# The context tile first in attention's last v part, the queries' rope table behind it, and unread products at the front of a hybrid block

## The chip, the cores and the metric

The kernel runs on one core of one Trainium2 chip. The metric is the device time of one execution in microseconds (us), the median over the runs shown. A core has TensorE (PE in the profile, its weight loads PEld), VectorE (DVE), ScalarE (ACT), GpSimd (POOL) and SyncE (SP), which issues the transfers between the main memory and the on-chip memory. Every engine works through its own list of instructions in order, and waits on semaphores for the others. TensorE writes into a small memory of eight banks (PSUM), from which VectorE and ScalarE fetch its results.

## The reference

One layer over 1024 latent tokens with a prefix of 256 context tokens, width 1024, batch 1, in float32:

```python
shift, scale, gate = split(silu(c) @ w_ada + b_ada, 3)          # and the same for c_ctx
h  = rms_norm(x)   * (1 + scale)   + shift
hc = rms_norm(ctx) * (1 + scale_c) + shift_c
qkv_a, z_a, a, b, q_b, k_b, v_b, z_b, gates = split_cols(h @ w_in)     # and of hc @ w_in
o_a = gdn_bidirectional(...)        # 8 heads of 128: short conv, gated delta rule, both directions
q = axial_rope(rms_norm(q_b)); k = concat(rms_norm(k_bc), axial_rope(rms_norm(k_b)))
v = concat(v_bc, v_b)
o_b = softmax(q0 k0) v - lam * softmax(q1 k1) v                 # 8 heads, two of 64 per head
y_a = rms_norm(o_a) * silu(z_a);  y_b = rms_norm(o_b) * (1 - lam0) * silu(z_b)
x = x + gate * ((g_a * (y_a @ w_oa) + g_b * (y_b @ w_ob)) @ w_out)
```

Rope turns pairs of a row's channels by an angle of the token's grid position; its cosines and sines, with the norm's gain in them, are a table that this kernel computes early, once for k and once for q, and keeps in the main memory (`tbd`).

## The kernel before, in words

All large products are made in three passes: each operand is split into a high part of fewer bits and a low part (the rest), and high x high, high x low, low x high are summed in a bank. `hs` holds the normalized, modulated h, transposed (channels on the partitions), as a high and a low tile for each of three groups of tokens: latent tiles 0 to 3, latent tiles 4 to 7, and the context's two tiles (group 2). `wh` and `wl` are a weight's high and low part, made from the raw load `wr`.

Before the program runs, a planner writes the order: each piece of work is a generator (a stream) that yields (engine, estimated us, what it depends on, what to emit), and `flow` or `turn_flow` picks the next step by the planner's own estimates of time. So a change of one stream can move the rows of others, and the engines then execute the order as it was written.

**The front** (`front`, L243) runs streams side by side. `loads` issues on SyncE: the constants `ct` (identity and two triangles, 128 x 384), c and c_ctx (`rows`), four tiles of x, the first weights, the first pair of w_ada's pieces (`wa`, 1 MB each), small vectors (`rw`), four tiles of x, three more pairs of `wa`, the context. `modulation` (L332) applies silu to c, transposes it (`tp<-ct,sil`), and for each of four pairs makes 8 small products of each piece (`mp<-wa,pad`, the "pads" below, each 32 columns of the array wide), copies the result (`mrow`; the first piece's on VectorE, the second's on ScalarE), and sums it by two "fold" products (`mp<-fold,mrow`), from which `mods` (shift and scale) comes. `rms` squares and sums each tile of x on ScalarE (`junk`), makes the inverse root on GpSimd and scales x on VectorE. `turns` transposes x (`pt<-ct,x`), and `turned` makes h's high part on ScalarE (`hs`, L407), h again on VectorE (`hf`, L410) and the low part on VectorE or GpSimd (L413). `main` (L417) makes the first 256 columns of the projection from them, the first `mm` products. `bank` (L238) hands out one of three banks for the front's transposes and modulation.

**The middle.** The convolution's projections follow, and then attention's k, v and q are projected in ten parts of 256 columns: four of k, two of v, four of q (`parts` in `run`), while the gated delta rule (GDN) runs beside them. `part_flow` (L937) makes the products of a part, two tiles of tokens (512 x 256 values, 48 products of 256 columns) at a time; k and v have ten tiles, the two of the context last, q has eight. `part_out` (L963) fetches a bank: for v a high and a low part (`vt`, L971 and L972), which SyncE stores (`vd`); for k and q a copy (`raw`), squares (`sq`). `part_post` (L989) then makes the norm's factor (`rsq`, L994, L995, and a power on GpSimd, L179) and six rope operations on VectorE (`sq`, `fin`, L1005 to L1007, two halves of three), four transposes on TensorE (`tr<-ct,fin`), two parts (`col`) and the stores (`qd`).

The queries' table is loaded into `hx`, whose buffer (tag `s20`) is that of the context's high part of h: its load (L947) must wait until the last product that reads the context is done. In the kernel before that is the last tile of the second v part, right ahead of the first q part. SyncE issues in order, so whatever stands behind a waiting request waits too.

Of the kernel before, what the change touches and what calls it, by code (L numbers as in the profile page):

```python
# [8 lines left out]
F32 = mybir.dt.float32  # L9
# [8 lines left out]
P = 128  # L18
D = 1024
KT = D // P  # L20
L = 1024
LC = 256
LT = L + LC
NT = LT // P
NL = L // P
# [9 lines left out]
PE, DVE, ACT, POOL, DMA, ADMA, DV2, PL1 = range(8)  # L35
# [8 lines left out]
class Block:  # L44
# [150 lines left out]
    def setup(self):  # L195
        nc, a = self.nc, self.a
        cp = self.cp = self.pool("const")
        self.dp = self.pool("spill", space=DRAM)
        ct = cp.tile([P, 3, P], F32, name="ct")
        nc.sync.dma_start(ct, a["consts"].rearrange("(a p) n -> p a n", p=P))  # L200
        self.ident, self.up, self.lo = (ct[:, i, :] for i in range(3))
        self.one = self.lo[:, 0:1]
        self.mhalf = cp.tile([P, 1], F32, name="mhalf")
        nc.gpsimd.memset(self.mhalf, -0.5)
        self.da = self.dp.tile([H, 2 * NT, 4, 32, 32], F32, name="da")
        self.db = self.dp.tile([H, 2 * NT, 4, 32, 32], F32, name="db")
        self.ya = self.dp.tile([2, H, P, L], F32, name="ya")
        self.yb = self.dp.tile([H, P, L], F32, name="yb")
        self.gkq = self.dp.tile([H, P, LT + L], F32, name="gkq")
        self.gkk = self.dp.tile([H, LT, P], F32, name="gkk")  # L210
        self.gv = self.dp.tile([H, LT, P], F32, name="gv")
        self.sza = self.dp.tile([H, P, L], F32, name="sza")
        self.szb = self.dp.tile([H, P, L], F32, name="szb")
        self.qd = self.dp.tile([2, H, P, L], F32, name="qd")
        self.kd = self.dp.tile([2, H, P, LT], F32, name="kd")
        self.vd = self.dp.tile([2, LT, H * P], F32, name="vd")
        self.gt = self.dp.tile([2 * KT, P, L], F32, name="gt")
        self.ma = self.dp.tile([KT, P, L], F32, name="ma")
        self.xq = self.dp.tile([H, P, 2, NT // 2, 2, 2, P], F32, name="xq")
        self.tbd = self.dp.tile([2, P, 1024], F32, name="tbd")  # L220
        self.gcd = self.dp.tile([2, H, LT], F32, name="gcd")
        self.gad = self.dp.tile([1, D], F32, name="gad")
        self.rbd = self.dp.tile([H, L], F32, name="rbd")
        for n in ("gkq", "gkk", "gv", "sza", "szb", "qd", "kd", "vd", "gt", "gcd", "ya", "yb"):
            self.dbg[n] = getattr(self, n).name
# [17 lines left out]
    def front(self, st, early, kv0):  # L243
# [5 lines left out]
        xt, wa, raws, T = {}, {}, {}, {}  # L249
# [82 lines left out]
        def modulation():  # L332
            sil = fs.tile([16, P], F32, name="sil")
            yield lambda: "rows" in T
            t = yield ACT, 0.3, T["rows"], lambda: nc.scalar.activation(sil, rows, AF.Silu), AF.Silu
            ib, tb, tp = self.bank("tp")
            t = yield PE, 0.2, [t, tb], lambda: self.tr(tp[:, 0:16], sil)
            tc = yield DVE, 0.15, [t], lambda: V.tensor_copy(cT, tp[:, 0:16])
            self.pfree.append((ib, tc))
            tz = yield PL1, 0.3, [], lambda: nc.gpsimd.memset(pad, 0.0)  # L340
            tc = yield DVE, 0.15, [tz, tc], lambda: V.tensor_copy(pad[:, :, 0:2].rearrange("p k s -> p s k"), c2)
            mrow = fs.tile([P, 2, W], F32, name="mrow")
            for u in range(4):
                yield lambda: ("wa", u, 0) in T and self.pfree
                ib, tb, mp = self.bank("mp")
                m = mods[:, :, 2 * u:2 * u + 2]
                bias = smallT[:, 0:16].rearrange("p (i k) -> p i k", i=2)[:, :, 2 * u:2 * u + 2]
                te = []
                for i in range(2):
                    yield lambda: ("wa", u, i) in T  # L350
                    o = i * W
                    for k in range(KT):
                        j = k % 4
                        t = yield PE, 0.08, [T["wa", u, i], tc, tb], lambda: self.mm(
                            mp[32 * j:32 * j + 32, o:o + W], pad[:, k], wa[u, i][:, k], k < 4, k >= 4)
                    if i:
                        t = yield ACT, 0.35, [t], lambda: nc.scalar.copy(mrow[:, i], mp[:, o:o + W])
                    else:
                        t = yield DVE, 0.42, [t], lambda: V.tensor_copy(mrow[:, i], mp[:, o:o + W])
                    for q in range(2):  # L360
                        t1 = yield PE, 0.17, [t], lambda: self.mm(
                            mp[:, o + 2 * q:o + 2 * q + 2], mrow[:, i, q * P:q * P + P], self.fold[:, 0:2])
                    te.append(t1)
                T["mm", u] = t
                yield lambda: "small" in T
                t = yield DVE, 0.17, [te, T["small"]], lambda: V.tensor_tensor(
                    m, mp.rearrange("p (i x) -> p i x", i=2)[:, :, 0:4].rearrange("p i (k s) -> p i k s", k=2),
                    bias.unsqueeze(3).to_broadcast([P, 2, 2, 2]), ALU.add)
                self.pfree.append((ib, t))
                T["m", u] = t  # L370
# [46 lines left out]
        def main():  # L417
            pts = [self.pm.tile([P, 512], F32, tag="mm", name="mm") for _ in range(5)]
            for g, ks in ORDER:
                n = len(groups[g]) * P  # L420
                for s, k in [(s, k) for s in range(2) for k in ks]:
                    yield lambda: ("h", g, k) in T and ("w", k // 4) in T
                    th, tl, _ = self.hsel(groups[g][0])
                    pt = pts[4][:, s * W:s * W + W] if g == 2 else pts[2 * s + g]
                    for i, (wt, ht) in enumerate(((0, th), (0, tl), (1, th))):
                        e = yield PE, 0.2265 if n == 512 else 0.1195, [T["h", g, k], T["w", k // 4]], lambda: self.mm(
                            pt, T["hl"][wt][:, k, s * P:(s + 1) * P], ht[:, k, :n], k == i == 0, k == KT - 1 and i == 2)
                    if k == KT - 1:
                        self.first_[s, g] = pt, e
            self.parts_done, self.part_t[0] = 1, e  # L430
# [506 lines left out]
    def part_flow(self, parts):  # L937

        self.free, self.nb = [None, None], 0
        free = self.free  # L940
        for i, (kind, pair) in enumerate(parts):
            yield lambda: i in self.parts_
            hi, lo, tw = self.parts_.pop(i)
            if parts[i - 1][0] != kind == "q":
                self.hx = self.hc.tile([P, 2, L], F32, tag="s20", name="hx")
                self.rope["q"] = self.hx[:, 0].rearrange("p (a b t f) -> p a b t f", a=2, b=2, f=32), (
                    yield DMA, 1.5, [self.part_t[i - 1]], lambda: self.nc.sync.dma_start(self.hx[:, 0], self.tbd[0]))  # L947
            for t0 in range(0, NL if kind == "q" else NT, 2):
                yield lambda: len(free) > self.nb
                pt = self.pm.tile([P, 512], F32, tag="mm", name="mm")  # L950
                for j in range(2):
                    th, tl, o = self.hsel(t0 + j)
                    m = 0
                    for k in range(KT):
                        for ht, wt in ((th, hi), (th, lo), (tl, hi)):
                            t = yield PE, 0.1195, [free[self.nb], tw], lambda: self.mm(
                                pt[:, j * W:j * W + W], ht[:, k, o:o + P], wt[:, k], m == 0, m == 3 * KT - 1)
                            m += 1
                self.evacs.append(self.part_out(kind, pair, t0, pt, t, free, self.nb))
                self.nb += 1  # L960
            self.parts_done, self.part_t[i] = i + 1, t

    def part_out(self, kind, pair, t0, pt, t, free, n):  # L963

# [24 lines left out]
    def part_post(self, kind, pair, t0, raw, sq, tr, t, s):  # L989

        nc, tk, V, Q = self.nc, self.tk, self.nc.vector, self.nc.gpsimd
        g, (tb, tt) = self.rope["g"], self.rope[kind]
        ss = self.rsq[:, t0:t0 + 2, 4 * pair:4 * pair + 4] if kind == "q" else tk.tile([P, 2, 4], F32, tag=f"ss{s}", name="ss")
        t = yield DVE, 0.6, [t], lambda: V.tensor_reduce(ss, sq.rearrange("p (t g d) -> p t g d", t=2, d=64), AX.X, ALU.add)  # L994
# [478 lines left out]
    def lam_setup(self):  # L1473
# [15 lines left out]
        self.dg = cp.tile([P, 1], F32, name="dg")  # L1489
        yield DVE, 0.15, [], lambda: V.tensor_scalar_mul(self.dg, self.diff_g, 1.0 - LAM0)  # L1490

    ISSUE = 0.5
    SPI = 0.5
    MW = 0.0
# [728 lines left out]
```

## Time and profile before

| | |
|---|---|
| three runs | 1931.37, 1928.17, 1931.5 us (median 1931.37) |
| the profiled execution | 1929.92 us, its span 1927.8 us |
| TensorE busy | 1885.5 us, 98% of the span |
| VectorE, ScalarE, GpSimd busy | 75%, 56%, 35% |
| the front (until the first transfers behind it) | 0 to 70 us |
| the v part that is changed, and the first q part | about 590 to 655 us |

A row of a timeline gives the start in us, the time from the group's first start to its last end in us, the engine, the line, the operation with output <- inputs, the partitions and shape, the count, and in brackets the idle time of the engine just before it and what ended it. A fp32 product of full precision stands there as two records. A row of the waits gives the engine and what it waited for, the total in us, the times and the longest. In the chain of waits a row is the start, the time and the piece. A row of a window gives its length, each engine's busy time (TensorE, its weight loads, VectorE, ScalarE, GpSimd) and instructions, the granted clock, the share of the transfer engines and GB/s.

### The profile page before, as it was taken

To read this page: it belongs to the slowest core of one execution; us is meant where nothing else is said; L and a number is where in the kernel's file an instruction comes from. 1 tells how busy PE (TensorE), PEld (TensorE's weight loads), DVE (VectorE), ACT (ScalarE), POOL (GpSimd) and SP (SyncE) were. 2 spreads that over 40 slices of the span, in tenths; PEclk is the share of its full clock that TensorE was granted. 3 is DMA by queue.
4 is the path that set the end of the run, shared out by engine and by line. 5 is a ranking of instruction groups with operands and counts; after the bars stand their busy time and mean duration, and the time that the engine had idled before them with its cause. 6 is when DMAs were issued, how large, how long until landed. Compare 5 with 4: busy or idle time off the path is not lost.

```text
span 1927.8 us, 37500 instructions
## 1 busy us (share of the span) xinstructions
PE 1885.5 (98%) x13807; PEld 1659.8 (86%) x13807; DVE 1446.3 (75%) x3613; ACT 1076.1 (56%) x2237; POOL 678.3 (35%) x610
## 2 busy tenths in 40 slices
PE   6999999999999999999999999999999999999999
PEld 4888888899999998888888888888997888888887
DVE  4697998957887887867865865338996979995677
ACT  4543444426233563677576656448885868884222
POOL 3200000005441342343333332326766667672203
PEclk9999999999999999999999999999999999999999
DMA  9144535575545557666785565666436474226542
GB/s 335 56 140 97 137 95 138 123 190 179 168 148 186 176 189 231 229 195 226 216 292 175 196 199 159 214 229 224 130 124 207 160 242 155 84 88 216 190 152 87
DMA packets 383039, 336.39 MB, mean 174 GB/s; under 512 B 142610, under 2 KB 323444, under 8 KB 381832
## 3 DMA queue, kind: packets, MB, share of 16 engines
q1 hardware_dynamic: 382855, 333.99, 55.2%
q8 instruction: 109, 1.79, 0.4%
q14 instruction: 75, 0.61, 0.1%
HBM read 222.14 MB, written 111.79 MB: 173 GB/s over the span
## 4 chain that ended last, share of the span: by engine, by line
PE 80%; DVE 7%; DMA 5%; ACT 4%; issue 2%; POOL 1%; SPq 1%; ACTq 0%; DVEq 0%; POOLq 0%
PE mm L56 40%; PE s L56 7%; PE v L56 5%; PE chain L56 5%; PE mb L56 5%; PE ma L56 4%; PE x L56 3%; PE t L63 3%; PE out L56 3%; PE gram L56 1%; DVE S L1579 1%; DMA sk<-gkq 1%; DVE ac L601 1%; PE tr L63 1%; PE mp L56 1%
## 5 line engine op out<-in xcount | busy, mean ns | idle before, releaser
L56 PE MATMUL mm<-hs,wh 128*128 128x512 f32 (+1 forms) x2048 | 648.6, 390 | 1.5 <-DVE hs L413 1.4
L56 PEld LDWEIGHTS mm<-hs,wh 128*128 128x128 f32 x2048 | 371.3, 189 | 58.9 <-DVE hs L413 1.9
L56 PE MATMUL mm<-hs,wl 128*128 128x512 f32 (+1 forms) x1024 | 397.6, 388 | 1.0 <-POOL wl L893 1.0
L56 PE MATMUL mm<-wh,hs 128*128 128x256 f32 (+1 forms) x1792 | 327.3, 283 | 0.3 <-ACT sq L985 0.3
L56 PEld LDWEIGHTS mm<-wh,hs 128*128 128x128 f32 x1792 | 276.8, 188 | 0.8 <-ACT sq L985 0.5
L1579 DVE TENSOR_SCALAR_CACHE_REDUCE S<-s,rsq 128x512 f32<-128x512 f32 (+1 forms) x384 | 239.5, 654 | 27.6 <-DMA vl<-vd 12.6
L56 PE MATMUL mm<-wl,hs 128*128 128x256 f32 (+1 forms) x896 | 253.3, 283 | 0.0
L1616 POOL TENSOR_TENSOR S<-S 128x1280 f32<-128x1280 f32 x64 | 189.1, 2958 | 91.9 <-ACT S L1609 90.6
L56 PEld LDWEIGHTS mm<-hs,wl 128*128 128x128 f32 x1024 | 193.9, 189 | 29.9 <-POOL wl L893 1.4
L1592 ACT ACTIVATE S<-S,mn 128x1280 f32<-128x1280 f32 x128 | 175.2, 1372 | 51.4 <-DVE mn L1591 51.3
L56 PEld LDWEIGHTS mm<-wl,hs 128*128 128x128 f32 x896 | 168.6, 188 | 0.1
L601 DVE SCALAR_TENSOR_TENSOR ac<-xc,convT,ac 128x1284 f32<-128x1284 f32 (+1 forms) x96 | 138.6, 1447 | 11.3 <-ACT ac L599 10.7
L56 PE MATMUL s<-kk,qh 128*128 128x512 f32 (+1 forms) x384 | 142.6, 372 | 1.9 <-DVE S L1579 1.7
L56 PE MATMUL s<-kk,ql 128*128 128x512 f32 (+1 forms) x384 | 133.0, 358 | 0.4 <-DMA ql<-qd 0.4
L1653 DVE TENSOR_TENSOR al<-t,ah 128x512 fp32r<-128x512 f32 (+1 forms) x192 | 106.8, 594 | 7.4 <-ACT ah L1648 6.0
L586 POOL MEMSET xc<- 128x2 f32 (+1 forms) x64 | 3.6, 101 | 297.3 <-ACT sq L635 113.8
L1167 DVE TENSOR_TENSOR ts<-ts,tmp 80x31 f32<-80x31 f32 (+15 forms) x248 | 92.2, 372 | 6.0
L1334 ACT ACTIVATE vd<-chain,edk 128x128 f32<-128x128 f32 x144 | 52.2, 370 | 76.9 <-PE chain L56 71.1
L56 PE MATMUL ma<-y,wh 128*128 128x512 f32 x256 | 93.0, 409 | 1.8 <-DVE g L1826 1.8
L1165 DVE TENSOR_TENSOR tmp<-ab,ts 80x31 f32<-80x31 f32 (+15 forms) x248 | 89.4, 360 | 6.4 <-DMA ab<-da 1.1
L1648 ACT CAST ah<-t 128x512 fp32r<-128x512 f32 (+1 forms) x192 | 88.1, 522 | 9.0 <-PE t L63 8.5
L56 PE MATMUL v<-al,vh 128*128 128x256 f32 x320 | 90.2, 282 | 0.7 <-DVE al L1653 0.6
(296 smaller groups left out, 4302.6 us busy)
## 6 DMA issues: line engine op xcount, KB each, us to landing
wr<-in_w_in_dram SPq DMA_DIRECT2D x48, 512.0 KB, 5.8
hx<-in_w_in_dram SPq DMA_DIRECT2D x64, 256.0 KB, 4.0
x<-xq SPq DMA_DIRECT2D x64, 256.0 KB, 4.8
X<-gcd SPq DMA_DIRECT2D x8, 1280.0 KB, 7.0
kd<-col SPq DMA_DIRECT2D x40, 256.0 KB, 2.1
xq<-X SPq DMA_DIRECT2D x16, 640.0 KB, 8.9
kk<-kd SPq DMA_DIRECT2D x16, 640.0 KB, 6.4
kq<-gkq SPq DMA_DIRECT2D x8, 1152.0 KB
```

What stands on the lines that cost most here:

```text
L56: self.nc.tensor.matmul(out, lhsT, rhs, start=start, stop=stop)
L63: self.nc.tensor.transpose(out, src, self.ident[:src.shape[0], :src.shape[0]])
L586: x["e"].append((yield PL1, 0.1, [old], lambda: nc.gpsimd.memset(xc[:, a:b], 0.0)))
L601: t = yield DV2, 1.21e-3 * wd, [t], lambda: nc.vector.scalar_tensor_tensor(ac[:, :wd], xc[:, j:j + wd], self.convw(j, x["ct"]), ac[:, :wd] ...
L1165: t = yield DV2, n * w / 960.0 + 0.08, [t if j else self.later(t, 2.5), t1], lambda: V.tensor_tensor(tv, ab[:, j + 1:, j:j + 1].to_broadca ...
L1167: t = yield DV2, n * w / 960.0 + 0.08, [t, t1], lambda: V.tensor_tensor(ts[:, j + 1:, :w], ts[:, j + 1:, :w], tv, ALU.subtract)
L1334: td = yield ACT, 0.251, [t], lambda: nc.scalar.activation(vd, pc[:, 1], AF.Copy, scale=self.edk[:, c, g:g + 1])
L1579: e = yield DVE, 0.675 if m == 512 else 0.408, [e, self.sfree[c].get(n - 4 + c)], lambda: self.nc.vector.tensor_scalar(x["S"][c][:, o:o + ...
L1592: x["x"].append((yield ACT, 1.36, [e], lambda: nc.scalar.activation(S, S, AF.Exp, bias=x["mn"][:, c:c + 1], scale=-1.0, accum_out=w["l0"][ ...
L1616: e = yield POOL, 2.9, [e], lambda: self.nc.gpsimd.tensor_tensor(S0, S0, S1, ALU.add)
L1648: e = yield ACT, 0.48 if nb == 4 else 0.27, [t, y["old", k]], lambda: self.nc.scalar.copy(y["ah", k][:, :, q], pv)
L1653: t = yield DVE, 0.603 if k < 2 else 0.322, [e, y["old", k]], lambda: self.nc.vector.tensor_tensor(y["al", k][:, :, q], pv, y["ah", k][:, ...
```

## The change

Four things, in two places.

At the front, 12 products of the identity with all of `ct` (128 x 384, fp32, unsplit) are put right behind the transpose of silu(c), into the bank that the first pads take later; the pads overwrite it, and nobody reads it. Three more (`WARM // 4`) stand behind the very first product of `main`, into a bank whose use comes later.

In the part that stands ahead of the first q part (the second of v), the context's two tiles are made first and the eight latent ones behind them. The load of the queries' table becomes a stream of its own (`query_table`, through the queue `asides`) that is opened behind the context tile and depends on its last product. `part_post` asks the planner to wait until the table's load has been placed.

```diff
@@ setup
+        self.ct = ct.rearrange("p a n -> p (a n)")
@@ modulation
             ib, tb, tp = self.bank("tp")
-            t = yield PE, 0.2, [t, tb], lambda: self.tr(tp[:, 0:16], sil)
+            held = self.bank("mp")
+            t = yield PE, 0.2, [t, tb], lambda: (self.tr(tp[:, 0:16], sil), self.mms((held[2][:, :3 * P], self.ident, self.ct) for _ in range(self.WARM)))
...
-                yield lambda: ("wa", u, 0) in T and self.pfree
-                ib, tb, mp = self.bank("mp")
+                yield lambda: ("wa", u, 0) in T and (held or self.pfree)
+                (ib, tb, mp), held = held or self.bank("mp"), None
@@ main
                             pt, T["hl"][wt][:, k, s * P:(s + 1) * P], ht[:, k, :n], k == i == 0, k == KT - 1 and i == 2)
+                        if g == s == k == i == 0:
+                            self.mms((pts[4][:, :3 * P], self.ident, self.ct) for _ in range(self.WARM // 4))
@@ part_flow
-            if parts[i - 1][0] != kind == "q":
-                self.hx = self.hc.tile([P, 2, L], F32, tag="s20", name="hx")
-                self.rope["q"] = self.hx[:, 0].rearrange("p (a b t f) -> p a b t f", a=2, b=2, f=32), (
-                    yield DMA, 1.5, [self.part_t[i - 1]], lambda: self.nc.sync.dma_start(self.hx[:, 0], self.tbd[0]))
-            for t0 in range(0, NL if kind == "q" else NT, 2):
+            last = kind != "q" and parts[i + 1][0] == "q"
+            for t0 in (NL, *range(0, NL, 2)) if last else range(0, NL if kind == "q" else NT, 2):
...
+                if last and t0 == NL:
+                    self.asides.append(self.query_table(t))
             self.parts_done, self.part_t[i] = i + 1, t
+
+    def query_table(self, t):
+        self.hx = self.hc.tile([P, 2, L], F32, tag="s20", name="hx")
+        self.rope["q"] = self.hx[:, 0].rearrange("p (a b t f) -> p a b t f", a=2, b=2, f=32), (
+            yield DMA, 1.5, [t], lambda: self.nc.sync.dma_start(self.hx[:, 0], self.tbd[0]))
@@ part_post
+        yield lambda: kind in self.rope
@@ class
+    WARM = 12
```

TensorE at the front, before (`sil` is silu(c), `rw` the small vectors, `x` the tokens):

```order
L63 MATMUL tp<-ct,sil 128x16
L56 MATMUL mp<-wa,pad 32x256 x8
L56 MATMUL mp<-fold,mrow 128x2 x2
L56 MATMUL mp<-wa,pad 32x256 x8
...
L56 MATMUL mp<-fold,mrow 128x2 x2
L63 MATMUL pt<-ct,x 128x128 x8
L56 MATMUL mm<-hs,wh 128x512 x2
L56 MATMUL mm<-hs,wl 128x512
```

and of the change:

```order
L63 MATMUL tp<-ct,sil 128x16
L56 MATMUL mp<-ct 128x384 x12
L56 MATMUL mp<-wa,pad 32x256 x8
L56 MATMUL mp<-fold,mrow 128x2 x2
L56 MATMUL mp<-wa,pad 32x256 x8
...
L56 MATMUL mp<-fold,mrow 128x2 x2
L63 MATMUL pt<-ct,x 128x128 x8
L56 MATMUL mm<-hs,wh 128x512
L56 MATMUL mm<-ct 128x384 x3
L56 MATMUL mm<-hs,wh 128x512
L56 MATMUL mm<-hs,wl 128x512
```

The 15 products (`mp<-ct`, `mm<-ct`) are the only new rows at the front; the order around them, on the other engines too, is the same.

SyncE's queue around the last v part, before (`wr` raw weights, `X`, `kq`, `xq`, `db`, `RR` the GDN's):

```order
L888 DMA wr<-in_w_in_dram 128x4x256 x2
L976 DMA vd<-vt 128x2x256 x8
L1247 DMA xq<-X 128x5x256 x2
L976 DMA vd<-vt 128x2x256 x2
L1097 DMA X<-gcd 128x2x1280
L1104 DMA kq<-gkq 128x2304
L888 DMA wr<-in_w_in_dram 128x4x256 x2
L947 DMA hx<-tbd 128x1024
L976 DMA vd<-vt 128x2x256 x2
L1169 DMA db<-ts 80x1024
```

and of the change:

```order
L892 DMA wr<-in_w_in_dram 128x4x256 x2
L985 DMA vd<-vt 128x2x256 x4
L970 DMA hx<-tbd 128x1024
L985 DMA vd<-vt 128x2x256 x4
L1257 DMA xq<-X 128x5x256 x2
L985 DMA vd<-vt 128x2x256 x2
L1107 DMA X<-gcd 128x2x1280
L1114 DMA kq<-gkq 128x2304
L892 DMA wr<-in_w_in_dram 128x4x256 x2
L985 DMA vd<-vt 128x2x256 x2
L1179 DMA db<-ts 80x1024
```

The table's load (`hx<-tbd`) has moved ahead of ten requests. On TensorE the queries' first four transposes stand 30 products earlier, and three other groups of transposes and Gram products within the q parts move by a few products; from there on the rows of every engine are in the order of before.

## The prediction

> **What bounds the kernel now.** First the page: busy shares, and the granted clock of the 40 slices.
>
> ```profile
> PE 1885.5 (98%) x13807; PEld 1659.8 (86%) x13807; DVE 1446.3 (75%) x3613; ACT 1076.1 (56%) x2237; POOL 678.3 (35%) x610
> PEclk9999999999999999999999999999999999999999
> ```
>
> TensorE is idle for 42.3 us in all, so what it gains anywhere should reach the end. The list of its waits has 17 us of these in the first 110 us (the three largest first below), and little from 640 to 760 us, just behind the second edit (last two):
>
> ```profile
> PE mp L56 <- DMA wa<-in_w_ada_dram: 8.9, 1, 8.9
> PE tp L63 <- ACT sil L335: 5.9, 1, 5.9
> PE mm L56 <- DVE hs L413: 1.4, 1, 1.4
> ...
> PE chain L56 <- DVE r L1325: 1.3, 1, 1.3
> PE tr L63 <- DVE Z L1228: 0.4, 1, 0.4
> ```
>
> Busy time hides something, though. TensorE's groups by form, up to 31 us (first two rows) and from 32 to 62 us (last two), show the same instructions at nearly half the duration later:
>
> ```profile
> L56 PE MATMUL mp<-wa,pad 128*32 128x256 f32 x48 | 5.8, 633 | 8.9 <-DMA wa<-in_w_ada_dram 8.9
> L56 PE MATMUL mm<-hs,wh 128*128 128x512 f32 x4 | 3.0, 753 | 1.5 <-DVE hs L413 1.4
> ...
> L56 PE MATMUL mm<-hs,wh 128*128 128x512 f32 x45 | 15.7, 413 | 0.0
> L56 PE MATMUL mp<-wa,pad 128*32 128x256 f32 x80 | 5.4, 385 | 0.0
> ```
>
> The granted clock reads 9 in the first slice too, so the slow state must be read from durations. The timeline of TensorE shows when it ends:
>
> ```profile
> 5.93 0.28 PE L63 MATMUL tp<-ct,sil 16*128 16x16 f32 x1 [5.93 <-ACT sil L335]
> 15.13 1.93 PE L56 MATMUL mp<-wa,pad 128*32 128x256 f32 x16 [8.92 <-DMA wa<-in_w_ada_dram]
> 18.55 1.93 PE L56 MATMUL mp<-wa,pad 128*32 128x256 f32 x16
> 23.87 0.80 PE L56 MATMUL mm<-hs,wh 128*128 128x512 f32 x1
> 26.11 0.79 PE L56 MATMUL mm<-hs,wh 128*128 128x512 f32 x1 [1.44 <-DVE hs L413]
> 31.94 0.39 PE L56 MATMUL mm<-hs,wl 128*128 128x512 f32 x1
> 32.50 0.51 PE L56 MATMUL mp<-fold,mrow 128*128 128x2 f32 x4
> 33.21 1.07 PE L56 MATMUL mp<-wa,pad 128*32 128x256 f32 x16
> ```
>
> Everything from 15.13 to about 31 us runs slow, and the rate doubles some 5 us after TensorE has become continuous at 26.11. That is the only rise the trace has.
>
> **The warming products.** Twelve unread products (128 x 384, fp32) go behind the transpose that ends at 6.2 us, three more behind the first product of the projection. Their price comes from the one full-size fp32 product in the trace and from the pads in the chain of waits (slow, then fast):
>
> ```profile
> 640.58 0.89 PE gram L56 x8
> ...
> 15.13 1.97 PE mp L56 x16
> ...
> 33.28 1.00 PE mp L56 x16
> ```
>
> Eight records are four products (two records each), 0.22 us per 128 columns: 0.67 us for 384 columns at the fast rate, and by 1.97/1.00 some 1.31 us at the slow one. If the rate rises after 5 us as above, at 11.2, 3.8 products are slow and 8.2 fast (5.5 us): the twelve end near 16.7, 1.6 us after the first pads were ready to run. From here I go along the chain. It runs through ScalarE and VectorE as well:
>
> ```profile
> 20.55 0.37 ACT L357 COPY mrow<-mp 128x256 f32<-128x256 f32 x1 [7.24 <-PE mp L56]
> 20.82 1.06 ACT L386 ACTIVATE junk<-x 128x1024 bf16<-128x1024 f32 x1
> 23.06 1.55 ACT L407 ACTIVATE hs<-pt,mods 128x512 fp32r<-128x512 f32 x2
> ...
> 25.37 0.68 DVE L413 TENSOR_TENSOR hs<-hf,hs 128x512 fp32r<-128x512 f32 x1
> 30.03 0.75 DVE L390 TENSOR_SCALAR x<-x,xry 128x1024 f32<-128x1024 f32 x1 [0.77 <-POOL xry L179]
> 30.70 0.42 DVE L359 COPY mrow<-mp 128x256 f32<-128x256 f32 x1
> ```
>
> First pads 16.7 to 17.7, copy and fold to 18.6, second pads 18.6 to 19.6 (before, 18.55 to 20.5). ScalarE's copy of them (20.55) then comes near 19.7, and all that ScalarE and, behind it, VectorE do in order from there comes 0.85 us earlier: the normalizing passes (20.82), the first half of h (23.06), its low part (25.37), the last scaling of x (30.03). The three extra products take 2.0 us at the fast rate and lie in the 1.44 us wait at 24.67 plus the 0.4 us that the first product saves there: nothing. The copy at 30.70 ends at 31.12 before, yet its fold ran at 32.50, because TensorE's slow backlog stood ahead of it; at the fast rate that backlog (eight products, one group of pads, six transposes: 3.5 us from 25.3) is gone by 28.8, so the fold follows the copy, now at 30.3. Beyond it both kernels run at the fast rate and TensorE has no wait until 62 us: **-2.2 us**.
>
> Loads cap it. The queue is full there:
>
> ```profile
> 0.00:10.00 10.00, 0.28 (x1) 0.18 (x1) 2.38 (x8) 5.24 (x9) 2.68 (x11) 1.00 0.76 268
> 10.00:20.00 10.00, 4.33 (x36) 2.20 (x36) 4.41 (x6) 2.93 (x4) 2.21 (x4) 1.00 1.08 396
> ```
>
> 2.68 MB by 10 us and 396 GB/s from there bring the second pads' weights (5.45 MB into the queue) at about 17.0 and the sixth tile of x (6.6 MB) at 19.9, an estimate from these rows. Were the twelve done by 15.1, the fold would come at 29.2: -3.3 at most. Each us by which the twelve end after 16.7 costs one: nothing is left at 18.9.
>
> The Trainium skill (TensorE: Matmul & The Clock Gate, Part 1) says the array runs at half clock until about 3.4 us of sustained work, against the 5 us of the row. By it the twelve end at 15.9 and this term is -3.0.
>
> **The rope table.** VectorE, the queue, TensorE and ScalarE around the queries' first tile:
>
> ```profile
> 628.57 0.17 DVE L995 TENSOR_SCALAR rsq<-rsq 128x8 f32<-128x8 f32 x1
> 632.49 0.42 DVE L1005 TENSOR_TENSOR sq<-raw,hx 128x256 f32<-128x256 f32 x1 [3.75 <-DMA hx<-tbd]
> 633.29 2.50 DVE L1007 TENSOR_TENSOR fin<-fin,sq 128x256 f32<-128x256 f32 x1
> ...
> 638.89 0.42 DVE L1005 TENSOR_TENSOR sq<-raw,hx 128x256 f32<-128x256 f32 x1
> 641.15 1.22 DVE L893 TENSOR_TENSOR wl<-wr,wh 128x1024 fp32r<-128x1024 f32 x1
> ...
> 621.17 11.30 DMA hx<-tbd
> ...
> 593.65 0.59 ACT L971 CAST vt<-mm 128x512 fp32r<-128x512 f32 x1 [1.39 <-PE mm L56]
> ...
> 636.97 0.66 PE L63 MATMUL tr<-ct,fin 128*128 128x128 f32 x4 [1.86 <-DVE fin L1007]
> ...
> 633.77 0.40 PE L56 MATMUL mm<-wh,hs 128*128 128x256 f32 x2
> 634.12 0.40 PE L56 MATMUL mm<-wh,hs 128*128 128x256 f32 x2
> ```
>
> The table is asked for at 621.17, when the context tile (last of the part) has left its buffer, and lands 11.3 us later. VectorE waits 3.75 us for it, TensorE 1.86. Now the context tile is the part's first; the tile in that place was cast at 593.65, so the request goes out near 594 and even after 11.3 us lies there 23 us before 628.74. VectorE's six rope operations then follow at once; they took 2.3 us (638.89 to 641.15) where nothing disturbed them: ready at 631.1. TensorE reaches the transposes 30 products earlier in the new order, at 0.118 us each (633.77 to 634.12 is three): 635.11 - 3.5 = 631.6. It does not wait: **-1.9 us**, with 0.5 us to spare. The bounds are 0 and -2.3 (the 1.86 and the 0.4 for Z above). The request passes ten others on SyncE's queue and holds up none: behind it stand stores whose data come later. The other order of the v tiles costs nothing, since the context's h was loaded at the front. TensorE's work is otherwise unchanged.
>
> **The sum.** -2.2 - 1.9 = -4.1 on the profiled execution's 1929.92 us (span 1927.8 and 2.1 around it): 1925.8. That execution lies 1.45 below the median of the three runs, 1931.37; from the median it is 1927.3. I say 1926.3, between them.
>
> **Rivals.** *The clock falls back.* From 19.6 to 23 us TensorE has only folds and transposes, and from 15.13 to 24.67 such work and pads never raised the rate. No row tells whether they hold it. If it is slow again at 23.0, the three products cost 3.9 us and end at 27.4, the rate rises at 28, the backlog is done at 31.4 and the fold comes 1.1 us early instead of 2.2: -3.0 in all, 1927.0. The same page of the Trainium skill is on this side: a gap of about 3 us throttles again (Part 1), and transposes do not count as busy (Part 4).
>
> *The table was not what was late.* VectorE's rope operations could meet GpSimd's subtraction, as the 2.50 us one did, or ScalarE's copies come late; then TensorE waits 1 to 2 us all the same, and only the front is left: 1927.7. For it speaks the margin of 0.5 us, against it that the 2.50 us one falls after 631.1.
>
> *The products delay what they were to speed up; slower.* If full fp32 products of constants do not raise the rate at all, the twelve last 15.7 us and end at 21.9. The pads that could start at 15.13 wait 6.8 us on the same in-order engine, ScalarE and VectorE behind them; the fold comes near 38.0, 5.4 us late: +3.5 in all, 1933.4. It decides from an end of the twelve at 20.8 on (16.7 + 2.2 + 1.9). Against it: the rate did rise within 5 us of dense products.
>
> **How the numbers follow.** Forecast 48%, clock falls back 22%, table without effect 15%, slow products 8%, neither edit felt 7% (about 1929.5). One measurement tells 0.2% (3.9 us) from no change. The forecast lies just beyond that: about two thirds of its 48 count as faster, a third of the second case and a quarter of the third: 42%. Slower takes half of the fourth and some noise: 5%; the rest, 53%, is no change. Range 1922.5 (both caps, -5.6, below the profiled time, less the runs' own scatter) to 1931.0 (neither felt, near the median); it leaves out the slow products. The forecast's own range is 1923 to 1928.5.
>
> **What would show it.** In the changed profile: the twelve end at 16 to 17.5 us, with durations that halve near 11; the pads from then on take 1.07 us, not 1.93; the fold of the second pair is at 30 to 31 instead of 32.50. The table's request stands near 594, VectorE has no wait on it, and TensorE's 1.86 us ahead of the transposes is gone. I am wrong if pads or the three products run slow behind the twelve, if the first pads start after 18.9, or if waits of TensorE later in the program grow by what was won.

## The result, and the profile after

The changed kernel took 1925.47 us (median of 9 runs, 1921.91 to 1928.97) against 1929.68 of the kernel before beside it (9 runs, 1928.03 to 1932.26): a ratio of 0.9974, 95% interval 0.9965 to 0.9983, 4.2 us by the medians. Predicted were 1926.3 us and 4.1 us less. The profiled execution has a span of 1923.8 us, before 1927.8.

The page, for the shares of the engines, and the list of TensorE's waits in the first 110 us:

```profile
PE 1891.4 (98%) x13837; PEld 1663.2 (86%) x13837; DVE 1450.3 (75%) x3613; ACT 1074.6 (56%) x2237; POOL 678.7 (35%) x610
...
PE tp L63 <- ACT sil L336: 6.0, 1, 6.0
PE mm L56 <- ACT hs L409: 1.2, 1, 1.2
PE pt L63 <- DVE x L392: 1.0, 3, 0.5
PE mp L56 <- DVE mrow L361: 0.5, 1, 0.5
```

TensorE is busy for 5.9 us more, though the kernel is shorter. The 8.9 us wait for w_ada's first piece is gone because the products fill it, so busy time says nothing here. The timeline of TensorE at the front says more:

```profile
6.03 0.28 PE L63 MATMUL tp<-ct,sil 16*128 16x16 f32 x1 [6.03 <-ACT sil L336]
6.25 10.72 PE L56 MATMUL mp<-ct 128*128 128x384 f32 x24
16.89 1.07 PE L56 MATMUL mp<-wa,pad 128*32 128x256 f32 x16
18.51 0.61 PE L56 MATMUL mp<-fold,mrow 128*128 128x2 f32 x4 [0.55 <-DVE mrow L361]
19.05 1.07 PE L56 MATMUL mp<-wa,pad 128*32 128x256 f32 x16
...
23.51 0.50 PE L56 MATMUL mm<-hs,wh 128*128 128x512 f32 x1 [1.20 <-ACT hs L409]
23.84 2.10 PE L56 MATMUL mm<-ct 128*128 128x384 f32 x6
...
30.79 0.56 PE L56 MATMUL mp<-fold,mrow 128*128 128x2 f32 x4
31.55 1.07 PE L56 MATMUL mp<-wa,pad 128*32 128x256 f32 x16
```

The twelve (24 records) make way for the pads at 16.89; pads take 1.07 us from the first group on, where they took 1.93; the second pair's fold stands at 30.79 instead of 32.50. Now SyncE, VectorE and TensorE around the queries' first tiles, and TensorE's fifth group of such transposes:

```profile
595.00 0.45 SPq L970 DMA_DIRECT2D hx<-tbd  x1
...
628.95 0.42 DVE L1015 TENSOR_TENSOR sq<-raw,hx 128x256 f32<-128x256 f32 x1
...
631.63 0.60 PE L63 MATMUL tr<-ct,fin 128*128 128x128 f32 x4
...
661.33 0.63 PE L63 MATMUL tr<-ct,fin 128*128 128x128 f32 x4 [1.00 <-DVE fin L1017]
```

The table is asked for 26 us earlier, VectorE no longer waits for it (no bracket at 628.95) and TensorE no longer waits ahead of the first transposes (none at 631.63). The wait of 1.00 us at 661.33, the fifth such group of transposes, is larger than before (0.10 us, too little for a bracket in the row):

```profile
663.22 0.66 PE L63 MATMUL tr<-ct,fin 128*128 128x128 f32 x4
```

Instruction by instruction (the median difference of the starts on VectorE and ScalarE), the change leads by 1.7 us at 40 to 100 us, 0.4 at 140 to 580, 1.7 at 640, 0.7 at 660 to 750, 2.4 from 760, 4.0 at 890, 2.7 behind 1100 and 4.0 from 1300 to the end. That is not two steps of 2 us. One pair of executions could not tell which of these steps belong to the change, so the two parts were run apart.

### The profile page after: what moved, and what is told of

It reads as the page before. It is cut to its first block, busy times and chain, and to the rows that moved or that the text cites. A ratio compares the mean times of both kernels' runs of the same rounds, so it can differ in the third digit from the quotient of the medians.

```text
span 1923.8 us, 37565 instructions
## 1 busy us (share of the span) xinstructions
PE 1891.4 (98%) x13837; PEld 1663.2 (86%) x13837; DVE 1450.3 (75%) x3613; ACT 1074.6 (56%) x2237; POOL 678.7 (35%) x610
## 4 chain that ended last, share of the span: by engine, by line
PE 57%; DVE 5%; ACT 2%; issue 1%; DMA 1%; POOL 1%; SPq 0%; ACTq 0%; DVEq 0%; POOLq 0%
PE mm L56 18%; PE s L56 7%; PE v L56 5%; PE chain L56 5%; PE mb L56 5%; PE ma L56 4%; PE x L56 3%; PE t L63 3%; PE out L56 3%; DVE S L1590 1%; PE gram L56 1%; DVE al L1664 1%; PE z L56 1%; ACT S L1603 0%; DMA kk<-gkk 0%
## 5 line engine op out<-in xcount | busy, mean ns | idle before, releaser
L605 DVE SCALAR_TENSOR_TENSOR ac<-xc,convT,ac 128x1284 f32<-128x1284 f32 (+1 forms) x96 | 138.5, 1447 | 11.9 <-ACT ac L603 11.3
```

The costliest lines, as they stand in the source:

```text
L605: t = yield DV2, 1.21e-3 * wd, [t], lambda: nc.vector.scalar_tensor_tensor(ac[:, :wd], xc[:, j:j + wd], self.convw(j, x["ct"]), ac[:, :wd] ...
```

## The experiments

Twelve kernels ran, in three groups of four on one chip each; every group had its own runs of the kernel before (33, 33 and 27).

**The kernel before once more**, for the scatter:

> The kernel before, unchanged, for a second trace and the scatter. Both theories: ratio 1.000. If the places where the two traces drift apart behind 700 us (0.4 us of wait on a load at 757, 1.6 us on another at 864) are chance, this trace differs from the first at such places too, by 1 to 2 us either way; if the change made them, it does not.

Measured 1930.32 us, 1.0006 (0.9997 to 1.0014); the span of its profile is 1928.2 us. Its trace leads the first one by 1.0 us at 90 us and lags by 1.0 at 200 to 600. So steps of 1 to 2 us between two single traces prove nothing. Part of this one comes from the clock: behind a wait of 2.09 us for the gates of the GDN the granted clock (third from the end in the window's row) is 0.74, where the first trace waited 0.93 us and has 1.00, and the lag grows from 0.5 to 1.0 us. TensorE's timeline and the window:

```profile
140.46 0.60 PE L63 MATMUL trg<-ct,gcc 128*16 128x128 f32 x4 [2.09 <-ACT egl L857]
...
139.00:145.00 6.00, 4.54 (x19) 3.37 (x20) 6.00 (x7) 2.78 (x6) 0.00 (x0) 0.74 0.00 0
```

The 1.7 us step at 757 us between the first traces of the two kernels is of this kind too: it was a wait of 1.33 us in the first trace of the kernel before, and none of the 13 other traces has over 0.5 us there.

**The front alone**, run twice (`part_flow`, `part_post` as before):

```diff
+            held = self.bank("mp")
+            ... self.mms((held[2][:, :3 * P], self.ident, self.ct) for _ in range(self.WARM))   # 12
+            self.mms((pts[4][:, :3 * P], self.ident, self.ct) for _ in range(self.WARM // 4))   # 3
```

> The 15 unread products alone, the table as before. Theory P (the prediction: TensorE bounds everything, what it gains passes to the end): -2.0 us, ratio 0.9990. Theory A (absorbed: between 106 and 140 us a weight load and the gates behind it set the time, and only 0.4 of the 1.7 us won by 70 us is left there): -0.4 us, ratio 0.9998.

> The fifteen products alone, a second time. Theory P: 2.2 us less, 0.9989. Theory S: as its first run, 0.9996. Theory A (a weight load at 106 to 113 us takes up what TensorE gained before it): ratio 1.0000, with a lead of 1.7 to 2.4 us at 90 us and under 1 us at 140 us.

Measured 1929.02 us, 0.9996 (0.9986 to 1.0006), and 1929.38 us, 0.9995 (0.9987 to 1.0004): less than half of what was expected, twice, by the medians; both intervals still hold the 0.9990 and 0.9989 of theory P, so the times alone do not decide. The front itself did what was predicted. The timeline of TensorE in the second run:

```profile
5.49 9.70 PE L56 MATMUL mp<-ct 128*128 128x384 f32 x24
15.19 1.07 PE L56 MATMUL mp<-wa,pad 128*32 128x256 f32 x16
...
22.65 0.80 PE L56 MATMUL mm<-hs,wh 128*128 128x512 f32 x1 [1.34 <-ACT hs L409]
23.24 3.46 PE L56 MATMUL mm<-ct 128*128 128x384 f32 x6
...
30.24 0.51 PE L56 MATMUL mp<-fold,mrow 128*128 128x2 f32 x4
```

The fold is at 30.24, 2.3 us early (30.16 in the first run), although here the clock did fall back: the product at 22.65 takes 0.80 us and the three take 3.46. The lead at 40 to 100 us is 2.3 and 2.0 us, and behind the weight load that theory A names (at 200 us) still 1.8 and 1.3. The lead goes at 633 to 645 us. The timeline of TensorE there, and two windows of it (the number behind the engines' busy times, third from the end, is the granted clock):

```profile
636.45 0.66 PE L63 MATMUL tr<-ct,fin 128*128 128x128 f32 x4 [2.58 <-DVE fin L1011]
...
637.98 0.63 PE L56 MATMUL mm<-wh,hs 128*128 128x256 f32 x2
638.62 0.63 PE L56 MATMUL mm<-wh,hs 128*128 128x256 f32 x2
...
633.00:639.00 6.00, 3.42 (x22) 3.22 (x21) 5.33 (x11) 3.42 (x9) 2.83 (x2) 0.83 0.43 81
639.00:645.00 6.00, 6.00 (x48) 6.00 (x47) 5.09 (x12) 3.79 (x8) 0.10 (x1) 0.88 0.20 69
```

and of the kernel before:

```profile
638.06 0.40 PE L56 MATMUL mm<-wh,hs 128*128 128x256 f32 x2
638.41 0.40 PE L56 MATMUL mm<-wh,hs 128*128 128x256 f32 x2
...
633.00:639.00 6.00, 4.14 (x35) 3.93 (x35) 5.33 (x9) 4.15 (x11) 3.65 (x2) 1.00 0.45 93
639.00:645.00 6.00, 6.00 (x54) 6.00 (x53) 5.84 (x14) 4.09 (x10) 0.94 (x2) 1.00 0.37 131
```

Two things happened: TensorE waited 2.58 us for the rope table instead of 1.86 (2.34 in the first run), and after this longer wait the clock fell: the same pair of products takes 0.63 instead of 0.40 us, and the granted clock is 0.83 and 0.88. That costs 6 x 0.17 + 6 x 0.12 = 1.74 us; the first run's 0.82 and 0.89 give 1.74 as well. With the longer wait, 2.2 to 2.5 us are gone, as much as the front had won. In these traces the wait that the other half of the change removes is what ate the front's gain: at 645 us both lag by 1.0. Behind 750 us they lead again, by 0.9 and 2.9 us at the end, in part because the first trace of the kernel before has waits of its own at 757 and 864 us.

**The rope table alone**, run twice (the diff of `part_flow`, `query_table` and `part_post`, without the products):

> The context tile first and the table behind it alone, no unread products. Theory P: -1.9 us, ratio 0.9990. Theory A: nearly all of the whole change's -4.2 us, -3.7, ratio 0.9981. In the trace, both: no wait of TensorE ahead of the queries' first transposes.

> Context tile first and the table behind it, a second time. Theory P: 1.9 us less, 0.9990. Theory S: as its first run, 0.9998. If the wait for the table is as long in the kernel before as in its later profiles (2 to 3 us between 600 and 700 us), more: 0.9985.

Measured 1929.05 us, 0.9998 (0.9989 to 1.0007), and 1926.65 us, 0.9979 (0.9969 to 0.9990). The two intervals hardly overlap; the middle of the two is -2.2 us, near the 1.9 expected, but the size is known to no better than 1 us either way. The traces agree with each other: no wait ahead of the first transposes, and one of 0.9 and 0.8 us ahead of the fifth group. SyncE's and TensorE's rows of the second run (before: request at 621.17, 1.86 us of wait):

```profile
598.03 0.42 SPq L967 DMA_DIRECT2D hx<-tbd  x1
...
632.93 0.60 PE L63 MATMUL tr<-ct,fin 128*128 128x128 f32 x4
```

The mean granted clock that stands beside each timed run is 1.000 in 19 of these 20 runs. Of the 93 runs of the kernel before it is 1.000 in 67, and the other 26 are 1.0 to 1.9 us longer (means of the three groups: 1929.2, 1930.0 and 1929.8 us at 1.000, 1931.2, 1931.0 and 1931.3 below). That would fit a clock that the kernel before loses at the table now and then, but it is not shown. Of that kernel's two traces one has a fall, and it is at 142 us (above); and of the 12 runs of the table's edit with the three products (below), which has no wait ahead of the first transposes in its trace either, 4 are below 1.000.

**The context tile first, the table not earlier.** The same tiles in the same order, but the request behind the whole part:

```diff
-                if last and t0 == NL:
+            if last:
                     self.asides.append(self.query_table(t))
```

> The context tile first, but the table asked for only when the whole part is done, at its old place in the queue. Both theories: ratio 1.000, and TensorE's 1.9 us of wait ahead of the first transposes is there as before; if the order of the tiles had a price or a gain of its own, it would show here.

Measured 1929.78 us, 0.9998 (0.9989 to 1.0006). SyncE and TensorE:

```profile
622.64 3.68 SPq L967 DMA_DIRECT2D hx<-tbd  x1
...
638.38 0.66 PE L63 MATMUL tr<-ct,fin 128*128 128x128 f32 x4 [1.59 <-DVE fin L1014]
```

The wait is there as before. What works is the early request; the order of the tiles only makes it possible.

**The number of products**: twelve without the three, twenty-four with the three, eight with the three, and the three alone.

```diff
-    WARM = 12
+    WARM = 12 / 24 / 8 / 0
-                            self.mms(... for _ in range(self.WARM // 4))
+                            (none) / range(3) / range(3) / range(3)
```

> The twelve products alone, without the three behind the first product; the table as before. If the three only fill a wait: as the 15 products alone (-2.0 us by theory P, -0.4 by theory A), fast rows throughout from 17 us. If they hold the clock up: rows slow again behind 24 us, and at most 1 us left of what is won by 70 us.

> 24 products in place of 12 (and the three); the table as before. They end near 24.6 instead of 16.9; at 1 us for each us, the fold of the second pair's first piece comes at 38.5 instead of 32.5 before: +6.0 us at 70 us and at the end, ratio 1.0031, by theory P. By theory A a delay is partly absorbed too where a load sets the time: +4.5.

> 8 products in place of 12 (and the three); the table as before. They end near 14.3, ahead of the first pads' weights. If the clock stays up: the second pads' load is the cap and 2.5 to 3.0 us are won by 70 us. If 2.3 us of fast products are too few to hold it: slow rows again by 20 us. At the end, theory P -2.7 us, ratio 0.9986; theory A -0.4.

> Only the three products behind the first product of the projection, none at the transpose; the table as before. At the slow rate they take 3.9 us against a wait of 1.4, and make TensorE continuous from 23.9 instead of 26.1: if 5 us of full-size work raise the clock, it rises near 29 instead of 31, and the second product starts at 28.1 instead of 26.1. Within 0.5 us of before at 70 us and at the end, ratio 0.9998.

| | start of the second pair's fold | TensorE's wait for the table | time | ratio (95%) |
|---|---|---|---|---|
| none (kernel before; fold and wait of its first trace) | 32.50 | 1.86 | 1929.93 | 1 |
| twelve | 31.52 | 2.58 | 1929.35 | 0.9998 (0.9989 to 1.0006) |
| 24 + 3 | 37.57 | 1.89 | 1933.25 | 1.0017 (1.0008 to 1.0026) |
| 8 + 3 | 31.27 | 2.52 | 1930.64 | 1.0000 (0.9991 to 1.0008) |
| 3 | 31.94 | 0.79 | 1928.22 | 0.9990 (0.9981 to 1.0000) |

At the front the 24 and the twelve behave as the chain of the prediction has it. The 24 last until 23.4 us, and the pads that could run at 15 us stand behind them; of the twelve without the three, the clock is lost again before the projection. With the eight it is lost sooner: the first pads take 1.07 us, the second again 1.93 (at 18.10 us), and instead of 2.5 to 3.0 us the fold gains 1.2. TensorE's timelines, first of the 24, then of the twelve:

```profile
5.92 17.48 PE L56 MATMUL mp<-ct 128*128 128x384 f32 x48
23.33 1.07 PE L56 MATMUL mp<-wa,pad 128*32 128x256 f32 x16
...
37.57 0.51 PE L56 MATMUL mp<-fold,mrow 128*128 128x2 f32 x4
```

```profile
23.45 0.79 PE L56 MATMUL mm<-hs,wh 128*128 128x512 f32 x1 [1.46 <-ACT hs L409]
25.61 0.80 PE L56 MATMUL mm<-hs,wh 128*128 128x512 f32 x1 [1.37 <-DVE hs L415]
...
27.19 1.94 PE L56 MATMUL mp<-wa,pad 128*32 128x256 f32 x16
...
31.52 0.51 PE L56 MATMUL mp<-fold,mrow 128*128 128x2 f32 x4
```

The 24 missed theory P's 1.0031: their fold is 5.1 us late, but the medians differ by 3.3 us and the interval ends at 1.0026. In their trace the lag is 5.7 us until 750 us and 1.4 to 1.8 from 1300 on; two of the steps between are the first trace's own waits at 757 and 864 us, so how much of a delay is made up again stays open.

With twelve or eight the table's wait is again 2.5 to 2.6 us, so these kernels wait 0.7 us longer at 636 us, and with the eight the clock fell there as well (below). The kernel with the three alone met a wait of 0.79 us in its trace and gained 1.7 us by the medians; whether that short wait comes from its timing or by chance is open, the more as the traced run is the longest of its ten (1931.67 us).

**The whole again, and the whole without its twelve**, beside the two parts on one chip:

> The whole change again, on one chip with its two parts (f2, f3). Theory P (both terms of the prediction reach the end): 4.1 us less than the kernel before, ratio 0.9979, and the sum of f2 and f3. Theory S (the parts as measured so far, 0.9996 and 0.9998, add up, and the first 0.9974 held chance of transfers that lie behind both edits): ratio 0.9994, 1 us less. In the trace either way: fold of the second pair at 30 to 31 us, no wait of TensorE ahead of the transposes of the queries' first tile.

> The change without its twelve products: context first, table behind it, and the three products alone. Theory P: the twelve are worth some 1.7 of the front's 2.2 us, so 2.4 us less than the kernel before, 0.9988, and 1.7 us behind f1. If the three alone bring the clock up (the 0.9990 of the three alone), and the twelve add nothing: equal to f1, 0.998 for both.

| same chip, before 1930.31 us | median | ratio (95%) |
|---|---|---|
| whole | 1924.95 | 0.9970 (0.9958 to 0.9981) |
| table alone | 1926.65 | 0.9979 (0.9969 to 0.9990) |
| table and the three | 1927.20 | 0.9980 (0.9972 to 0.9988) |
| front alone | 1929.38 | 0.9995 (0.9987 to 1.0004) |

Theory S falls: 0.9994 lies outside the interval of the whole, for the second time. Theory P's 0.9979 lies within both. With the wait for the table gone, the front adds 1.7 us (1926.65 to 1924.95), about the 1.5 and 1.7 us of lead that the whole's two traces have at 40 to 100 us; with the wait in place it added 0.6 to 0.9. These are medians, and the intervals overlap. Theory P also had the parts add up, and on this chip they do within the noise: 3.7 and 0.9 make 4.6 us, the whole has 5.4. That the parts hinder each other is therefore read from the traces of the front alone, not from the times. The twelve are needed for the front's part: the three with the table bring nothing beyond the table. Nothing that was run beats the whole change.

## Why the prediction was right, and where it was not

**The time and the sum were right**: 4.1 us predicted, 4.2 and 5.4 measured by the medians, in both runs with 4.1 inside the interval. The rows account for less. The front's lead in the whole's traces is 1.6 us, and at the table 1.9 us of wait are gone and some 0.6 come back (below): 2.9 us, an estimate from these rows, while the two intervals begin at 3.3 and 3.7 us less. What the rest is the runs do not show; that the sum came out so well is therefore in part luck. Two small things in the working were off and decide nothing. The forecast of 1926.3 counts from 0.5 us above the profiled time and the rivals' 1927.0 and 1927.7 count from that time itself, so these times lie 0.4 to 0.5 us closer to the forecast than their terms do. And the table's request passes twelve others on SyncE's queue, not ten.

**The warming products.** Predicted were an end at 16.7, pads of 1.07 us behind it, a fold at 30.3 and -2.2 us. Measured: 16.89, 1.07, 30.79 (30.71 in the second trace of the whole), and a lead of 1.7 and 1.5 us in the whole's two traces, 2.3 and 2.0 in the front's alone, 1.9 in the mean. The rise of the clock was priced well: a product takes two records of 0.64 us before 11.53 us and of 0.32 after, against 1.31 and 0.67 us a product in the prediction. That the rise came when it was expected is luck, though: from the start of the first product to the first shorter record it took 5.3 and 4.6 us in the whole's two traces (5 predicted from one rise), but 2.7 to 4.0 in the five other traces with such products. The half us that is missing in the whole is the step "copy and fold to 18.6, second pads 18.6 to 19.6": the pads ended 0.3 us later than that step assumes, TensorE waited 0.55 us for the copy and the fold took 0.61, so the second pads began at 19.05. ScalarE's copy of them came at 20.19 instead of 19.7, and the rest of the chain is as late.

**The clock falls back** was a rival at 22%. It is what happened in the traces of both fronts alone, of the twelve, the 24 and the eight; in both traces of the whole it did not. These two are not typical: their mean granted clock is 1.000, but 9 of the whole's 15 runs are below (0.997 to 0.999), as are 20 of the front's 23 and one of the table's 20. So the clock fell in most runs of the whole too; where, no trace shows, and these nine are 1.0 us longer in the mean than the other six. As a rival it was wrong in its price. In the front alone the three took 3.46 us, ended at 26.7 and the fold still came at 30.24, 2.3 us early, not 1.1. There silu's transpose came at 5.3 us instead of 6.0, and the rate rose sooner (the twelve took 9.70 us instead of 10.72), so the twelve ended 1.7 us earlier, and ScalarE and VectorE were about 0.9 us earlier from the first half of h on. The prediction had taken this start from one trace; it varies from 5.1 to 6.3 us.

**The rope table.** The request near 594 (595.00), VectorE's six operations without a wait from 628.95 on and done at 631.3 (631.1 predicted), TensorE there at 631.6 (631.63) without a wait: all as predicted. What was missed is the next wait in line. "TensorE's work is otherwise unchanged" and "it does not wait, with 0.5 us to spare" held for the first group alone: the fifth waits 0.8 to 1.0 us in all five traces with this edit, against 0 to 0.8 (mean 0.4) in the nine without. So some 0.6 us of the 1.9 come back as a wait that the prediction did not price.

**"What it gains anywhere should reach the end"** is the step that the traces of the front alone contradict. The table's wait is where an earlier TensorE gives its lead back: the front alone met 2.34 and 2.58 us there instead of 1.86. Part of it is the transfer, which took 12.0 and 12.1 us in these two traces against 11.3; why, they do not show. On top came what no step had: a wait of this length can cost twice, once while TensorE stands and then 1.74 us of lost clock. In these traces the two terms are therefore not independent: the second edit removes the place where the first one's gain was lost. The whole's two traces have neither the wait nor the fall there.

**The wait at the gates** (theory A: a weight load at 106 to 113 us takes up the front's lead) is not borne out. It looked so from the first pair of traces, 0.93 us before against 2.11 after. But the first trace of the kernel before was the short one. TensorE's timeline there, of the whole's second trace and of the table alone, which has nothing new at the front:

```profile
138.81 0.60 PE L63 MATMUL trg<-ct,gcc 128*16 128x128 f32 x4 [1.29 <-ACT egl L861]
```

```profile
141.00 0.60 PE L63 MATMUL trg<-ct,gcc 128*16 128x128 f32 x4 [1.77 <-ACT egl L858]
```

TensorE is idle between 110 and 145 us for 1.6 to 2.9 us without the front's edit (five traces, mean 2.2) and for 2.2 to 3.0 with it (four, mean 2.5).

**Open** stay the size of the table's part (0.9998 once, 0.9979 once) and whether a wait for a GDN load at 864 us belongs to it: it is 0.2 to 1.6 us in eight of the nine traces without this edit, and of the five with it four have none and one (the table and the three) 0.8; nothing in the prediction or the runs says why.

## What to carry to other kernels

Two small edits far apart can depend on each other: an earlier engine meets the next late transfer sooner, so before a gain is carried to the end, find the next wait on its way and ask whether the gain only makes that longer. A wait of TensorE between dense products is to be priced with what follows it; here those of 2.3 us and more cost nearly double in three traces of four, and one of 2.1 us did so once. And where two edits are worth 2 us each and two traces of one kernel differ by 1 to 2, the whole and its parts have to be run on one chip before single traces are read, and more often than the 6 to 12 times here if their sum is to be told from the whole.

## What the hardware showed unexpectedly

The clock falls in the middle of the program, too. Among the waits for the table, those of 2.34, 2.52 and 2.58 us (both fronts alone, and the eight) were followed by a granted clock of 0.78 to 0.93 over 12 us, worth 1.74 us each time; the twelve waited 2.58 us and kept 1.00. The five shorter ones, 0.79 to 1.89 us, had no such fall. Length alone does not decide: the kernel with the three alone stood 1.6 us at 596 us, in a stretch of small products, and was granted 0.95 and 0.93 from 580 to 610; and at the gates the change waited 2.11 us up to 139.56 us and kept 1.00, while the kernel before, run again, waited 2.09 us up to 140.46 us and was granted 0.74 over 6 us. The Trainium skill (TensorE: Matmul & The Clock Gate, Part 1) puts the idle time that throttles at about 3.4 us, seen through a window that runs freely. A window of that length at half clock would lose 1.7 us, an estimate from the page's figures, and the 1.74 agree with it; but the idle time needed here was shorter than the page says.

The granted clock of the profile shows a fall only after the clock has once been up. The kernel before reads 1.00 until 31 us, while its pads take 1.93 us instead of 1.07; the front alone reads 0.88 from 18 to 24 us, where its products slow down again. At the start of a kernel the rate has to be read from durations.
